# Recurrence steps with the heads in two column halves and the state used as it is; preparation products alternating between row halves

## The chip, the cores and the metric

The kernel runs on one core of a Trainium2 chip. The metric is the device time of one execution in microseconds (us). Times of engines come from one execution that the hardware profiler recorded.

## What is computed

A block of depth 2 on 512 latent and 256 context tokens (768 in all), width 1024, everything in fp32. Each layer computes a modulation from `ada_w`, a projection, then side by side an RWKV group (a recurrence in both directions over 8 heads of 64 channels, over the context and on into the latents) and a differential attention, an output projection and an MLP. The change touches the RWKV group alone:

```python
def step(state, inp):                       # one token
    r_t, w_t, k_t, v_t, kk_t, b_t = inp
    sa = jnp.einsum("bhvk,bhk->bhv", state, kk_t)
    state = (state * w_t[:, :, None, :]
             - sa[..., :, None] * b_t[:, :, None, :]
             + v_t[..., :, None] * k_t[:, :, None, :])
    y = jnp.einsum("bhvk,bhk->bhv", state, r_t)
    return state, y
...
for d, reverse in enumerate((False, True)):
    dec_c, km_c, b_c = direction_terms(kc, kkc, xwc, xac, w0[d], w_b[d], a0[d], a_b[d], k_a)
    state_c, yc = wkv_scan(state0, rc, dec_c, km_c, vc, kkc, b_c, reverse)
    _, yl = wkv_scan(state_c, r, dec, km, v, kk, bb, reverse)
```

## The kernel before

The tokens of a direction are cut in chunks of 64. A tile `n` (0 to 5) is 128 tokens of each direction `d`; a **step** `(n, j)` takes one chunk of both directions, so a layer has 12 steps and 24 calls (step and direction). Within a chunk the recurrence is a triangular system, and so it is solved by an inverse per chunk and head.

`prep_a` and `prep_b` are the **preparation** of one unit: tile `n`, direction `d`, four of the eight heads (`pp`). A unit projects the low-rank inputs (L977, out `pb`, with the zero-padded input `ltz`), makes decays by a sigmoid on GpSimd (`sg`), scans (`cs`) and exponentials, forms `BK` and `KR`, multiplies them to `G` (L1046: two PSUM banks one after the other, each the product over one half of the rows, four heads; each is evacuated by VectorE at L1048), and transposes `BK` into `BN` (L1053). `KR`, `BN` and `G` lie in one buffer `S` per tile and direction, of which there are six, so the buffer of tile n is used again by tile n+3. `relay` (L1086) sends the diagonal 32x32 blocks of `G` to DRAM (`da`).

`inv(n)` loads them as `N` and `W` (L1115, L1116), inverts all blocks of a tile at once by **elimination** (30 rounds of a product at L1100 and a sum at L1102, on GpSimd for n below 2 and on VectorE for the rest), sends the result out (`dn` L1123, `dt` L1127) and back (`TT` L1132, `Gs` L1137), and `merge(n)` fills the off-diagonal blocks of the inverse in `G`: 32 small products at L1152 and L1154, a copy `Z`, 32 products at L1160 and L1162, a copy on VectorE (L1164) and one on ScalarE (L1165).

A call of `step` on TensorE: `X` of 64 rows by 512 columns, the eight heads side by side, from `G` and the values `uv` (L1186, rows 64 to 127 of the array as contraction), plus the state's part by four products with a block-diagonal copy `sbd` of the state (L1189). ScalarE negates `X` into `xs` (L1192). The inverse in `G` times `xs` gives `us` (L1198), copied into `uv` (L1201). `BN` times `uv` gives the state's increment (L1210), VectorE adds and scales it (`st` L1213, `sc` L1215), and ScalarE copies it twice, by halves, into `sbd` (L1218). The output is summed up in rows 64 to 127 of `X`'s bank (L1226) and evacuated into `Y` (L1236, L1239). `finish` normalizes a token tile and transposes it (L1288).

Layer 0's preparation of tiles 0 and 1 and their inverses run beside the attention, the rest in `rest`: per n the inverse of n+1, the steps of n, the preparation of n+2, with TensorE matmuls of the modulation (`adar`, weights `in_ada_w` by DMA) and finished tiles' work between. This is only the order in which the code emits; a tile scheduler orders the instructions on each engine when the kernel is built, and each engine then runs its queue in that order. An fp32 matmul shows in the trace as two MATMUL records, a transpose as one.

Of the kernel before, what the change touches and what calls it, by code (L numbers as in the profile page):

```python
# [10 lines left out]
F32 = mybir.dt.float32  # L11
# [153 lines left out]
class K:  # L165
# [760 lines left out]
    def recurrence(self, l, last, es, side):  # L926
# [18 lines left out]
        ltz = [tp.tile([128, 2, 128], F32, name=self.n("ltz")) for _ in range(2)]  # L945

        for z in ltz:
            nc.gpsimd.memset(z, 0.0)
# [3 lines left out]
        sbd = one.tile([128, 2, 4, 128], F32, name=self.n("sbd"))  # L952
        nc.gpsimd.memset(sbd, 0.0)
        sc = [one.tile([128, 4, 64], F32, name=self.n("sc")) for _ in range(2)]
# [7 lines left out]
        def prep_a(n, d, pp):  # L962
# [3 lines left out]
            lt = ltz[d]  # L966
            if pp == 0:
                for a in range(2):
                    ps = slice(64 * a, 64 * a + 64)
                    nc.sync.dma_start(lt[ps, a, :], self.zd[16, ps, tok])  # L970
# [3 lines left out]
            pw = bank([128, 2, 2, 128])  # L974
# [6 lines left out]
            for p in range(2):  # L981
                nc.scalar.activation(th[:, p, :], pw[:, p, 0, :], AF.Tanh, scale=0.5,
                                     bias=self.Q(l, "w0h")[:, q + p:q + p + 1])
            for p in range(2):
                nc.scalar.activation(ta[:, p, :], pw[:, p, 1, :], AF.Tanh, scale=0.5,
                                     bias=self.Q(l, "a0h")[:, q + p:q + p + 1])
            return ld, th, ta

        def prep_b(n, d, pp, ld, th, ta):
# [51 lines left out]

            for hf in range(2):
                hs = slice(hf * 64, hf * 64 + 64)
                pgt = bank([128, 4, 128])
                for u in range(4):
                    nc.tensor.matmul(pgt[:, u, 0:nn], BK[hs, u, :], KR[hs, 2 * pp + u, 0:nn],  # L1046
                                     start=True, stop=True, skip_group_check=True)
                nc.vector.tensor_tensor(G[:, us, hf, 0:nn], pgt[:, :, 0:nn],  # L1048
# [118 lines left out]
        def step(n, j):  # L1167
            need_y = not (last and n < 2)
            final = n == 5 and j == 1
            mw = 128 if need_y else 64  # L1170
            S = []
            for d in range(2):
# [4 lines left out]
                self.gate = ld  # L1177
                KR, BN, G, dcv = sets[(n, d)]
                S.append(dict(q=q, t0=t0, uv=uv, KR=KR, BN=BN, G=G, dc=dcv))
            for d in range(2):  # L1180
                s = S[d]
                q = s["q"]
                X = s["X"] = px[d].tile([128, 512], F32, name=self.n("X"), tag=f"X{d}")
                for h in range(8):
                    w = mw if h == 0 else 64
                    nc.tensor.matmul(X[0:w, h * 64:h * 64 + 64], s["G"][64:128, h - h % 2 + q, h % 2, 0:w],  # L1186
                                     s["uv"][64:128, h, :], start=(h == 0), stop=False, skip_group_check=True)
# [4 lines left out]
                nc.scalar.mul(xs[0:64], X[0:64, :], -1.0)  # L1192
                yield
            for d in range(2):
                s = S[d]
                up = us[:, d]
                for h in range(8):
                    nc.tensor.matmul(up[(h % 2) * 64:(h % 2) * 64 + 64, h // 2, :], s["G"][:, h - h % 2 + s["q"], h % 2, 0:64],  # L1198
                                     s["xs"][:, h * 64:h * 64 + 64], start=True, stop=True, skip_group_check=True)
# [3 lines left out]
            if not final:  # L1203
                for d in range(2):
                    s = S[d]
                    q = s["q"]
                    sp = us[:, d]
                    for h in range(8):
                        hs = slice((h % 2) * 64, (h % 2) * 64 + 64)
                        nc.tensor.matmul(sp[hs, h // 2, :], s["BN"][:, h - h % 2 + q, hs], s["uv"][:, h, :],  # L1210
                                         start=True, stop=True, skip_group_check=True)
                    tt = uvp.tile([128, 4, 64], F32, name=self.n("st"), tag="st")
                    nc.vector.tensor_tensor(tt, sp, sc[d], ALU.add)  # L1213
                    dcv = s["dc"][:, q:8:2].unsqueeze(2).to_broadcast([128, 4, 64])
                    nc.vector.tensor_tensor(sc[d], tt, dcv, ALU.mult)  # L1215
                    for hf in range(2):
                        hs = slice(hf * 64, hf * 64 + 64)
                        nc.scalar.copy(sbd[hs, d, :, hs], sc[d][hs])  # L1218
                    yield
            if need_y:  # L1220
                for d in range(2):
                    s = S[d]
                    X = s["X"]
                    for h in range(8):
                        ks = slice(0, 64 if h == 0 else 128)
                        nc.tensor.matmul(X[64:128, h * 64:h * 64 + 64],  # L1226
                                         s["G"][ks, h - h % 2 + s["q"], h % 2, 64:128],
                                         s["uv"][ks, h, :], start=False, stop=(h == 7), skip_group_check=True)
# [4 lines left out]
                    yo = Yt[hp * 64:hp * 64 + 64, :]  # L1233
                    if hp not in seen:
                        seen[hp] = 1
                        nc.scalar.copy(yo, X[64:128, :])  # L1236
                    else:
                        seen[hp] = 2
                        nc.vector.tensor_tensor(yo, X[64:128, :], yo, ALU.add)  # L1239
# [4 lines left out]
        def finish(ti):  # L1244
# [40 lines left out]
            yield  # L1285
            pt = bank([128, 4, 128])
# [450 lines left out]
```

## Time and profile before

| what | value |
|---|---|
| three runs, median (lowest to highest) | 2450.8 us (2442.71 to 2458.3) |
| profiled execution: time; span; mean granted clock | 2465.64 us; 2463.9 us; 0.933 |
| busy over the span: PE, DVE, ACT, POOL | 92%, 62%, 48%, 33% |
| recurrence of layer 0, 494 to 763 us | 269 us, granted clock 0.90 |
| recurrence of layer 1, 1758 to 2062 us | 304 us, granted clock 0.77 |

The recurrence stretches reach from the end of the attention beside which the first tiles are prepared to the last products of the output projection that stand between steps. PE is TensorE's matmuls, DVE is VectorE, ACT ScalarE, POOL GpSimd, SP the queue that issues most DMAs.

### The profile page before, as it was taken

Reading aid. Unit: us, or ns where it says so; the run is one execution under the profiler, and the core shown is the slowest. Engines: PE = TensorE matmul, PEld = TensorE weight load, DVE = VectorE, ACT = ScalarE, POOL = GpSimd, SP = SyncE. Lnnn points to the kernel's source line nnn. Section 1 sums busy time; section 2 is a strip of 40 time slices with the busy share of each in tenths; the row PEclk is TensorE's granted clock in tenths of the full one; section 3 lists DMA queues with packets and bytes.
Section 4 is the critical chain, followed back from the end, with each engine's and each line's share of the span. In section 5 each row is a group of like instructions: output and inputs, shape, how many; then the busy total and the mean of one; then the engine's idle time right before and its main releaser. Section 6 shows DMA issues by size and latency. Waiting matters only on the chain.

```text
span 2463.9 us, 43744 instructions
## 1 busy us (share of the span) xinstructions
PE 2273.2 (92%) x17150; PEld 1919.2 (78%) x17150; DVE 1516.6 (62%) x2629; ACT 1173.8 (48%) x2393; POOL 806.8 (33%) x1048
## 2 busy tenths in 40 slices
PE   6999998799989999999999989999989978999997
PEld 5887887677768988888888877788767758888886
DVE  5456458558654665555555646657556564778784
ACT  4345547554534543344343535547444444555452
POOL 1212324832111333333330422423641131553530
PEclk8999998798899999999999999999678879999998
DMA  7543535386687422221112354434566663423230
GB/s 270 154 129 94 133 110 140 74 228 172 148 208 236 152 77 69 69 69 61 60 61 85 124 164 122 122 108 115 148 158 158 166 161 137 161 91 117 87 119 35
DMA packets 291630, 313.67 MB, mean 127 GB/s; under 512 B 139680, under 2 KB 220896, under 8 KB 291424
## 3 DMA queue, kind: packets, MB, share of 16 engines
q1 hardware_dynamic: 280320, 284.66, 38.6%
q0 software_dynamic: 10240, 23.08, 5.0%
q8 instruction: 135, 2.21, 0.4%
q10 hardware_dynamic: 864, 3.15, 0.3%
q14 instruction: 71, 0.58, 0.1%
HBM read 257.04 MB, written 53.77 MB: 126 GB/s over the span
## 4 chain that ended last, share of the span: by engine, by line
PE 68%; DMA 10%; DVE 9%; ACT 4%; issue 3%; SPq 2%; POOL 2%; POOLq 0%; DVEq 0%; ACTq 0%
PE pf L351 31%; PE pu L351 15%; PE po L351 4%; DMA raw<-in_ada_w 2%; PE pb L1046 2%; PE po L832 2%; DMA TT<-dt 2%; PE X L1186 1%; PE pb L977 1%; PE adar L265 1%; PE sc L795 1%; DVE wl L1497 1%; PE X L1226 1%; DVE nm L797 1%; PE X L1189 1%
## 5 line engine op out<-in xcount | busy, mean ns | idle before, releaser
L1497 DVE TENSOR_TENSOR wl<-raw,wh 128x1024 fp32r<-128x1024 f32 x170 | 255.8, 1507 | 125.6 <-ACT wh L1496 124.8
L351 PE MATMUL pf<-hl,wh 128*128 128x512 f32 (+1 forms) x832 | 282.1, 342 | 0.0
L351 PE MATMUL pf<-hh,wh 128*128 128x512 f32 (+1 forms) x832 | 280.5, 342 | 0.5 <-ACT hh L397 0.5
L351 PE MATMUL pf<-hh,wl 128*128 128x512 f32 (+1 forms) x832 | 275.7, 342 | 0.0
L1496 ACT ACTIVATE wh<-raw 128x1024 fp32r<-128x1024 f32 x170 | 179.2, 1058 | 162.0 <-PE pf L351 143.9
L351 PE MATMUL pf<-wh,fah 128*128 128x512 f32 x570 | 225.3, 398 | 11.5 <-DVE fu L1630 7.2
L351 PE MATMUL pu<-hh,wh 128*128 128x512 f32 (+1 forms) x632 | 223.5, 354 | 4.8 <-DVE t L557 1.7
L351 PE MATMUL pf<-wl,fah 128*128 128x512 f32 x570 | 225.0, 396 | 0.7 <-DVE wl L1497 0.7
L351 PE MATMUL pf<-wh,fal 128*128 128x512 f32 x570 | 222.8, 397 | 1.8 <-DVE fal L1597 1.8
L351 PE MATMUL pu<-hh,wl 128*128 128x512 f32 (+1 forms) x632 | 218.1, 346 | 4.4 <-DVE wl L340 4.4
L351 PE MATMUL pu<-hl,wh 128*128 128x512 f32 (+1 forms) x632 | 217.8, 345 | 0.0
L797 DVE TENSOR_REDUCE nm<-sc 128x1 f32<-128x768 f32 (+1 forms) x160 | 132.6, 842 | 79.2 <-PE sc L795 78.5
L351 PEld LDWEIGHTS pf<-hl,wh 128*128 128x128 f32 x832 | 156.6, 188 | 20.0 <-DVE hl L399 0.2
L351 PEld LDWEIGHTS pf<-hh,wl 128*128 128x128 f32 x832 | 156.0, 188 | 20.0
L351 PEld LDWEIGHTS pf<-hh,wh 128*128 128x128 f32 x832 | 155.3, 188 | 20.4 <-ACT hh L397 0.8
L799 ACT ACTIVATE e<-sc,nm 128x768 f32<-128x768 f32 (+1 forms) x160 | 130.7, 821 | 53.7 <-DVE nm L797 44.3
L321 POOL TENSOR_TENSOR rs<-ms,pw 128x1 f32<-128x1 f32 (+2 forms) x60 | 56.8, 948 | 286.3 <-DVE ms L319 284.5
L351 PEld LDWEIGHTS pu<-hh,wh 128*128 128x128 f32 x632 | 121.0, 191 | 23.8 <-DVE t L557 2.3
L351 PEld LDWEIGHTS pf<-wh,fah 128*128 128x128 f32 x570 | 107.7, 189 | 38.9 <-ACT fah L1596 13.7
L1630 DVE TENSOR_TENSOR acc<-pf,acc 128x512 f32<-128x512 f32 x155 | 104.2, 682 | 53.9 <-PE pf L351 53.3
L351 PEld LDWEIGHTS pu<-hh,wl 128*128 128x128 f32 x632 | 120.7, 191 | 19.5 <-DVE wl L340 5.3
L351 PEld LDWEIGHTS pu<-hl,wh 128*128 128x128 f32 x632 | 120.8, 191 | 14.2 <-issue 1.7
(262 smaller groups left out, 5644.1 us busy)
## 6 DMA issues: line engine op xcount, KB each, us to landing
raw<-in_w_ff SPq DMA_DIRECT2D x128, 512.0 KB, 3.7
raw<-in_ada_w SPq DMA_DIRECT2D x96, 512.0 KB, 5.8
raw<-in_w_in SPq DMA_DIRECT2D x52, 512.0 KB, 4.6
ld<-zd SPq DMA_DIRECT2D x40, 384.0 KB, 3.9
ks<-qd POOLq DMA_DIRECT2D x64, 192.0 KB, 5.8
zd<-zr SPq DMA_DIRECT2D x22, 384.0 KB
raw<-in_w_out SPq DMA_DIRECT2D x16, 512.0 KB, 5.9
qs<-qd POOLq DMA_DIRECT2D x32, 192.0 KB, 6.0
```

What stands on the lines that cost most here:

```text
L265: nc.tensor.matmul(acc[32 * g:32 * g + 32, :], self.sc[:, 2 * kp + k, :], raw[:, k, g * 128:g * 128 + 128], start=(kp + k == 0), stop=(kp ...
L321: nc.gpsimd.tensor_tensor(r, m, self.pw1.to_broadcast([128, cols]), ALU.pow)
L351: nc.tensor.matmul(out, a, b, start=(start and i == 0 and j == 0), stop=(i == n - 1 and j == 2), skip_group_check=not start)
L795: nc.tensor.matmul(sc[:, k0:k1], qs[:, br, tk], ks[:, br, k0:k1], start=True, stop=True)
L797: nc.vector.tensor_reduce(nm, sc, AX.X, ALU.max, negate=True)
L799: nc.scalar.activation(ee, sc, AF.Exp, bias=nm, accum_out=ls[:, br:br + 1])
L832: nc.tensor.matmul(po, pT[:, k * 128:k * 128 + 128], vn[:, k, h * 64:h * 64 + 64], start=(k == 0), stop=(k == nk - 1))
L977: nc.tensor.matmul(pw[:, p, :, :], wab[:, d, cs], lt, start=True, stop=True, skip_group_check=True)
L1046: nc.tensor.matmul(pgt[:, u, 0:nn], BK[hs, u, :], KR[hs, 2 * pp + u, 0:nn], start=True, stop=True, skip_group_check=True)
L1496: nc.scalar.activation(hi, src, AF.Copy)
L1497: nc.vector.tensor_tensor(lo, src, hi.bitcast(F32), sub)
L1630: nc.vector.tensor_tensor(d, p, d, add)
```

## The change

`lt` replaces the padded `ltz`: one DMA instead of two, no zeros, and four products with a contraction of 64 rows into two banks instead of two products of 128 rows and 256 columns into one. The `G` products run over the heads outside and the two row halves inside, so that both banks are held at once. `sbd` and its copies are gone: `from_state` multiplies the state `sc` as it is, head by head, in 64x64 products that alternate between the quadrants of the array, once for `X` and once more for the output. `X` is 128 rows by 4 heads, even heads in the upper column half, odd in the lower; its `G` product contracts all 128 rows, with `uv[0:64]` zeroed by a new memset on GpSimd, so it reads the rows of `G` that hold the inverse too. `xs` is two muls of 64x256. `us` and the state's increment lie in `X`'s bank, the output in a bank of its own (`Yb`). `finish` transposes by sixteen 64x64 products.

```diff
-        ltz = [tp.tile([128, 2, 128], F32, name=self.n("ltz")) for _ in range(2)]
+        lts = [tp.tile([128, 128], F32, name=self.n("lt")) for _ in range(2)]
...
+            pw = [bank([128, 2, 128]) for _ in range(2)]
             for p in range(2):
                 cs = slice((pp + p) * 128, (pp + p) * 128 + 128)
-                nc.tensor.matmul(pw[:, p, :, :], wab[:, d, cs], lt, start=True, stop=True, skip_group_check=True)
+                for a in range(2):
+                    ps = slice(64 * a, 64 * a + 64)
+                    nc.tensor.matmul(pw[a][:, p, :], wab[ps, d, cs], lt[ps, :], start=True, stop=True,
+                                     skip_group_check=True)
...
+            pgs = [bank([128, 4, 128]) for _ in range(2)]
+            for u in range(4):
+                for hf in range(2):
+                    hs = slice(hf * 64, hf * 64 + 64)
+                    nc.tensor.matmul(pgs[hf][:, u, 0:nn], BK[hs, u, :], KR[hs, 2 * pp + u, 0:nn],
+                                     start=True, stop=True, skip_group_check=True)
...
+                nc.gpsimd.memset(uv[0:64], 0.0)
...
+            def from_state(out, s, c0):
+                for h in range(8):
+                    hs = half(h)
+                    nc.tensor.matmul(out[hs, h // 2, :], s["KR"][hs, h - h % 2 + s["q"], c0:c0 + 64], s["old"][hs, h // 2, :],
+                                     start=False, stop=False, skip_group_check=True)
...
-                for p in range(4):
-                    nc.tensor.matmul(X[0:mw, p * 128:p * 128 + 128], s["KR"][:, 2 * p + q, 0:mw], sbd[:, d, p, :],
-                                     start=False, stop=False, skip_group_check=True)
+                    nc.tensor.matmul(X[half(h), 0, h // 2, :], s["G"][:, h - h % 2 + s["q"], h % 2, 0:64],
+                                     s["uv"][:, h, :], start=(h < 2), stop=False, skip_group_check=True)
+                from_state(X[:, 0], s, 0)
...
-                    for hf in range(2):
-                        hs = slice(hf * 64, hf * 64 + 64)
-                        nc.scalar.copy(sbd[hs, d, :, hs], sc[d][hs])
...
+                        nc.tensor.matmul(Y[half(h), h // 2, :], s["G"][:, h - h % 2 + s["q"], h % 2, 64:128],
+                                         s["uv"][:, h, :], start=(h < 2), stop=False, skip_group_check=True)
+                    from_state(Y, s, 64)
```

The order on the engines changes far beyond these lines. TensorE before, layer 0, at the merge of tile 2 (it writes `S_5374` and `S_5501`, the two directions of tile 2; X_6648 and X_6771 are this same tile's):

```order
L1189 MATMUL X_6648<-sbd_3609,S_5374 128x128 x4
L265 MATMUL adar_6685<-raw_6716,sc 32x128 x3
L1186 MATMUL X_6771<-uv_6646,S_5501 64x64 x3
L1046 MATMUL pb_6851<-S_4135,BK_6823 128x128 x4
L1046 MATMUL pb_6857<-S_4135,BK_6823 128x128 x4
L1189 MATMUL X_6771<-sbd_3609,S_5501 128x128 x4
L287 MATMUL adat_7084<-cst,row_6726 128x128
L977 MATMUL pb_6874<-ltz_3603,wab_3600 128x256 x2
L1152 MATMUL pg_5905<-TT_5898,S_5374 32x32
```

TensorE with the change, at the merge of the same tile (it writes `S_5401` and `S_5538`; `S_4146` and `S_4387` are tile 1, and X_6064 and X_6174 are tile 1's):

```order
L1186 MATMUL Yb_5857<-sc_5663,S_3920 64x64 x8
L1186 MATMUL X_6064<-sc_5825,S_4146 64x64
L265 MATMUL adar_6085<-raw_6096,sc 32x128 x7
L265 MATMUL adar_6085<-raw_6106,sc 32x128 x8
L265 MATMUL adar_6085<-raw_6116,sc 32x128 x8
L975 MATMUL pb_6130<-lt_3602,wab_3600 128x128
L975 MATMUL pb_6131<-lt_3602,wab_3600 128x128
L1045 MATMUL pb_6162<-S_3659,BK_6156 128x128 x4
L1193 MATMUL X_6174<-uv_6061,S_4387 64x64 x2
L1152 MATMUL pg_5988<-TT_5981,S_5401 32x32
```

The merge of tile n stood at the X products of tile n's first step, and now stands at those of tile n-1's first step, one tile earlier; all merges from tile 2 on stand so in layer 0, and nearly so in layer 1.

VectorE before, layer 0, about the merge copy of tile 2 (`W_6462` is the elimination of tile 3, BK and cs belong to the preparation of later tiles):

```order
L1100 TENSOR_TENSOR pr_6494<-W_6462,N_6461 128x105
L1102 TENSOR_TENSOR W_6462<-W_6462,pr_6494 128x5x21
L1100 TENSOR_TENSOR pr_6497<-W_6462,N_6461 128x120
L1102 TENSOR_TENSOR W_6462<-W_6462,pr_6497 128x6x20
L1100 TENSOR_TENSOR pr_6500<-W_6462,N_6461 128x114
L1102 TENSOR_TENSOR W_6462<-W_6462,pr_6500 128x6x19
L1294 TENSOR_TENSOR ysq_6664<-ysq_6664,frk_6662 128x512
L1100 TENSOR_TENSOR pr_6503<-W_6462,N_6461 128x126
L1164 COPY S_5374<-pg_5940 32x16x32
L1018 SCALAR_TENSOR_TENSOR cs_7462<-scm_3606,sg_7459 128x260
L1034 TENSOR_TENSOR BK_6995<-ta_6878,xi_6989 128x4x2x32
L1035 TENSOR_TENSOR BK_6995<-th_6877,xi_6989 128x4x64
```

VectorE with the change, the end of the elimination of tile 2 (`W_5876`) and the merge copy behind it:

```order
L1102 TENSOR_TENSOR W_5876<-W_5876,pr_5965 128x15x2
L1100 TENSOR_TENSOR pr_5968<-W_5876,N_5875 128x15
L1102 TENSOR_TENSOR W_5876<-W_5876,pr_5968 128x15
L1017 SCALAR_TENSOR_TENSOR cs_6217<-scm_3604,sg_6214 128x260
L1030 TENSOR_TENSOR th_6136<-th_6136,ld_6128 128x256
L1048 TENSOR_TENSOR S_3659<-pb_6162,cst 128x4x128
L1031 SCALAR_TENSOR_TENSOR ta_6137<-ta_6137,ld_6128 128x256
L1034 TENSOR_TENSOR BK_6227<-th_6136,xi_6221 128x4x64
L1033 TENSOR_TENSOR BK_6227<-ta_6137,xi_6221 128x4x64
L1048 TENSOR_TENSOR S_3659<-pb_6163,cst 128x4x128
L1164 COPY S_5401<-pg_6023 32x16x32
```

and further on the end of the preparation of tile 3 (`S_3920`) and the start of tile 3's elimination (`W_6611`):

```order
L1017 SCALAR_TENSOR_TENSOR cs_6902<-scm_3604,sg_6899 128x260
L1048 TENSOR_TENSOR S_3920<-pb_6372,cst 128x4x128
L1030 TENSOR_TENSOR th_6335<-th_6335,ld_6327 128x256
L1031 SCALAR_TENSOR_TENSOR ta_6336<-ta_6336,ld_6327 128x256
L1034 TENSOR_TENSOR BK_6912<-th_6335,xi_6906 128x4x64
L1033 TENSOR_TENSOR BK_6912<-ta_6336,xi_6906 128x4x64
L1048 TENSOR_TENSOR S_3920<-pb_6373,cst 128x4x128
L1241 TENSOR_TENSOR Y_5701<-Yb_6404,Y_5701 128x256
L1100 TENSOR_TENSOR pr_6616<-W_6611,N_6610 128x30
```

The elimination of tile n+1 was interleaved with the merge of tile n and with the preparation of tile n+2; now it stands behind that merge and behind its own tile's last three units of preparation (two of them between rows not shown here), nearly undivided.

TensorE with the change, `G` products of another unit (`pb_6243` and `pb_6244` are the two banks of one unit):

```order
L1204 MATMUL X_6064<-xs_5148,S_4146 64x64 x8
L1204 MATMUL X_6174<-xs_5149,S_4387 64x64 x2
L1045 MATMUL pb_6243<-S_3659,BK_6227 128x128 x4
L1045 MATMUL pb_6244<-S_3659,BK_6227 128x128 x4
L1053 MATMUL pb_6255<-cst,BK_6227 128x128 x4
L1204 MATMUL X_6174<-xs_5149,S_4387 64x64 x6
L1215 MATMUL X_6064<-uv_6058,S_4146 64x64 x2
```

The code emits the products of the two banks in turn; here the built order has all four of one and then all four of the other, as before at `pb_6851` and `pb_6857`.

## Rows read from the trace of the kernel before

**Rows 1.** Windows: busy us (instructions) per engine, granted clock, DMA share.

```profile
494.00:763.00 269.00, 240.41 (x3478) 192.92 (x3477) 169.22 (x461) 128.52 (x304) 66.12 (x113) 0.90 0.77 198
...
1758.00:2062.00 304.00, 260.51 (x3339) 215.35 (x3337) 167.99 (x453) 129.14 (x301) 88.18 (x178) 0.77 0.57 147
```

**Rows 2.** Chain of waits by line, the two recurrence stretches.

```profile
by line: DMA raw<-in_ada_w 10.1%; DMA TT<-dt 7.3%; PE pb L1046 6.5%; PE X L1226 6.1%; PE adar L265 5.8%; PE X L1186 4.1%; DMA raw<-in_w_out 3.5%; DMA S<-gd 3.3%; PE pb L977 3.2%; DMA da<-S 3.1%; PE X L1189 3.0%; issue 3.0%; PE us L1198 3.0%
...
by line: PE X L1186 8.5%; PE pb L1046 6.0%; PE adar L265 5.7%; PE X L1189 5.4%; PE po L351 5.3%; issue 4.8%; PE pb L977 4.7%; DMA TT<-dt 4.7%; DMA raw<-in_ada_w 4.3%; PE X L1226 4.1%; DMA S<-zd 3.9%; PE us L1198 3.5%; PE us L1210 2.8%; DVE 
```

**Rows 3.** Chain in order of time: start us, us, what (TensorE calls).

```profile
495.39 1.09 PE X L1189 x8
...
497.34 1.32 PE X L1186 x16
...
504.66 0.61 PE us L1198 x16
...
506.96 0.61 PE X L1226 x8
...
1760.33 1.89 PE X L1186 x16
```

**Rows 4.** Groups by line, whole program: busy us, mean ns.

```profile
L1102 DVE TENSOR_TENSOR W<-W,pr 128x30 f32<-128x30 f32 (+7 forms) x240 | 66.0, 275 | 5.5
L1100 DVE TENSOR_TENSOR pr<-W,N 128x30 f32<-128x30 f32 (+7 forms) x240 | 65.7, 274 | 15.5 <-DMA N<-da 10.3
```

**Rows 5.** Chain in order of time, from a relay to a merge.

```profile
566.46 5.18 DMA da<-S
...
574.71 6.68 DMA N<-da
...
637.57 3.99 DMA dn<-W
...
642.03 3.27 DMA TT<-dt
...
645.35 0.24 PE pg L1152 x2
```

**Rows 6.** Timeline of ScalarE, last copy of merges: start us, us.

```profile
530.70 0.58 ACT L1165 COPY S<-pg 32x512 f32<-32x512 f32 x1 [5.54 <-DVE S L1164]
...
733.74 0.58 ACT L1165 COPY S<-pg 32x512 f32<-32x512 f32 x1
...
1861.26 0.58 ACT L1165 COPY S<-pg 32x512 f32<-32x512 f32 x1 [4.27 <-DVE S L1164]
...
2024.90 0.58 ACT L1165 COPY S<-pg 32x512 f32<-32x512 f32 x1
```

**Rows 7.** Timeline of TensorE at a merge.

```profile
646.53 0.26 PE L1154 MATMUL pg<-TT,S 32*32 32x32 f32 x1
646.54 0.26 PE L1152 MATMUL pg<-TT,S 32*32 32x32 f32 x1
646.60 0.24 PE L1154 MATMUL pg<-TT,S 32*32 32x32 f32 x1
```

**Rows 8.** Timeline of TensorE, start of preparation units in layer 1.

```profile
1708.88 1.02 PE L977 MATMUL pb<-ltz,wab 128*128 128x256 f32 x4
...
1714.47 1.03 PE L977 MATMUL pb<-ltz,wab 128*128 128x256 f32 x4
...
1744.45 1.88 PE L977 MATMUL pb<-ltz,wab 128*128 128x256 f32 x4 [1.53 <-DVE S L1048]
...
1751.54 2.02 PE L977 MATMUL pb<-ltz,wab 128*128 128x256 f32 x4
```

**Rows 9.** Waits of TensorE: us in total, times, longest (stretches 494:770, 1760:2055).

```profile
PE adar L265 <- DMA raw<-in_ada_w: 15.0, 11, 2.6
PE X L1189 <- ACT sbd L1218: 3.1, 2, 2.2
...
PE pg L1152 <- DMA TT<-dt: 10.4, 5, 5.4
```

More of the change, by code (lines that the diff above doesn't have):

```diff
@@ L951, in recurrence @@
         nc.gpsimd.memset(scm[:, 0:260:65], 0.0)
-        sbd = one.tile([128, 2, 4, 128], F32, name=self.n("sbd"))
-        nc.gpsimd.memset(sbd, 0.0)
-        sc = [one.tile([128, 4, 64], F32, name=self.n("sc")) for _ in range(2)]
+        state = lambda d: one.tile([128, 4, 64], F32, name=self.n("sc"), tag=f"sc{d}", bufs=2)
+        sc = [state(d) for d in range(2)]
         for s in sc:
@@ L1040, in prep_b @@
             yield
-            for hf in range(2):
-                hs = slice(hf * 64, hf * 64 + 64)
[L1044 to L1048, printed above, removed]
+            pgs = [bank([128, 4, 128]) for _ in range(2)]
[4 more added lines that the diff above has]
+                                     start=True, stop=True, skip_group_check=True)
+            for hf in range(2):
+                nc.vector.tensor_tensor(G[:, us, hf, 0:nn], pgs[hf][:, :, 0:nn],
                                         msk[:, 0:nn].unsqueeze(1).to_broadcast([128, 4, nn]), ALU.mult)
@@ L1222, in step @@
                     s = S[d]
-                    X = s["X"]
+                    Y = yp.tile([128, 4, 64], F32, name=self.n("Yb"), tag="Yb")
                     for h in range(8):
[L1225 to L1228, printed above, removed]
+                        nc.tensor.matmul(Y[half(h), h // 2, :], s["G"][:, h - h % 2 + s["q"], h % 2, 64:128],
+                                         s["uv"][:, h, :], start=(h < 2), stop=False, skip_group_check=True)
+                    from_state(Y, s, 64)
                     ti, hp = s["t0"] // 128, (s["t0"] // 64) % 2
@@ L1287, in finish @@
             for p in range(4):
-                nc.tensor.transpose(pt[:, p, :], Yt[:, p * 128:p * 128 + 128], self.ident)
+                for hp in range(2):
+                    for hf in range(2):
+                        hs = slice(hf * 64, hf * 64 + 64)
+                        c0 = hp * 256 + p * 64
+                        nc.tensor.matmul(pt[hs, p, hp * 64:hp * 64 + 64], Yt[hs, c0:c0 + 64], self.ident[hs, hs],
+                                         start=True, stop=True, skip_group_check=True)
             o1 = sq.rearrange("p (j t) -> p j t", j=4)
@@ L1308, in rest @@
             uvp = self.pool(es, "uvp", 2)
-            xsd = [uvp.tile([128, 512], F32, name=self.n("xs"), bufs=1) for _ in range(2)]
+            xsd = [uvp.tile([128, 2, 4, 64], F32, name=self.n("xs"), bufs=1) for _ in range(2)]
             for x in xsd:
@@ L1314, in rest @@
             late["pg"] = lambda shape: pg.tile(shape, F32, name=self.n("pg"), tag="g")
-            us = self.pool(es, "pus", 1, PSUM).tile([128, 2, 4, 64], F32, name=self.n("us"))
+            yp = self.pool(es, "pyb", 1, PSUM)
             pms.append(self.pool(es, "pmr", 1, PSUM))
```

51 lines of the change are left out of this document (21 added, 30 removed).

## The prediction

> **What bounds the kernel now.** I read the busy times of the two recurrence stretches first [rows 1]. TensorE is busy 240 of 269 us in layer 0 and 261 of 304 us in layer 1, at granted clocks of 0.90 and 0.77; VectorE is busy 169 and 168 us, ScalarE some 129, GpSimd under 90. So TensorE looks like the bound. The chain of waits says less [rows 2]: no TensorE line has more than 8.5% of a stretch, and in layer 0 the first two entries are DMAs, one of them (TT<-dt) the last transfer of an inverse. The waits of TensorE name the same two sources, a modulation weight (15.0 us) and TT (10.4 us in layer 1) [rows 9]. Third, the last copies of the merges [rows 6]: from tile 1 to tile 5 they take 530.7 to 733.7 in layer 0, and from tile 2 to tile 5 1861.3 to 2024.9 in layer 1, which is most of each stretch. Steps can't run ahead of these. So there are two clocks in the stage, TensorE's work and the loop of preparation, relay, elimination and merge, and the question is which of them the new order leaves in charge.
>
> **What the change takes off TensorE.** A call's X was 1.32 us (products from one row half into one column half) and 1.09 us (block-diagonal state) [rows 3]. The new G product has the shape of the us product, alternating column halves over 128 rows: 0.61 us [rows 3]. The state's product, 64x64 in alternating quadrants, has no row. Its bounds are 0.3 us (half of 0.61, if the two row halves run beside each other) and 1.32 us (nothing beside anything, as in the old X); I take 0.61, since alternating column halves at least is the same. X falls from 2.41 to 1.22 us. The output falls from twice 0.61 [rows 3] to 0.61 for G, and rises by the second state product, another 0.61: no change. The relief is 1.19 us a call, 24 calls a layer: 29 us in layer 0 and, at a granted clock of 0.77, 37 us in layer 1, 66 together (27 to 83 by the two bounds). At half clock the old X piece was 1.89 us [rows 3], so the relief grows there too.
>
> The preparation should gain by products that alternate row halves, but the built order undoes most of it: where one G product follows another, it changes the bank in 88 of 305 places (39 of 313 before), and the low-rank products change in 48 places of 118. I give it 0 to -5 us. The dropped sbd copies free ScalarE of two copies a call; TensorE waited for them 3.1 us in layer 0 [rows 9], so that is all they are worth. The added memset of uv on GpSimd costs nothing while GpSimd is three quarters idle in layer 0 and 70% idle in layer 1 [rows 1]; without that cover, what stands behind it on the queue is the sigmoid and KR of a later unit. It must wait for a free uv buffer, as the uv load on SP does. From a gain of nothing to a loss of 1 us in each of 24 steps is the bound; I take 0. The finish's sixteen small transposes against four change under 1 us a tile.
>
> One thing in the order speaks against the alternation in the array. At a merge, a product at L1154 and one at L1152 start 0.01 us apart, from different row groups of 32 and into the same bank, and the next pair follows 0.06 us later, though one record takes 0.24 us [rows 7]. So here row groups run beside each other in one bank. The Trainium skill, TensorEngine Tiling (Array Packing), Restrictions and Gotchas, says that different row tiles can't access the same PSUM bank at the same time; from_state does precisely that, and by this rule its products would run one after the other. What that would give is the third rival.
>
> **What the change puts on the path.** In the built order the merge of tile n stood beside the X of tile n, which did not read the inverse; the new X contracts all 128 rows, reads what the merge writes, and the merge stands one tile earlier on TensorE. On VectorE the elimination of tile n+1 no longer overlaps the merge of tile n: behind the merge copy come the evacuations of three units' G (in layer 0; 2.5, 1.5 and 3 units in layer 1), and only then the 60 operations of the elimination, nearly undivided. A queue runs in order, so merge, units, relay, elimination and merge follow one another. One turn of this loop:
> - three units. Units began 5.6 us apart in the prologue of layer 1 at full clock [rows 8]. The first one's head stands ahead of the merge copy, so three take between two pitches, 11.2, and three, 16.8: 14.
> - relay. da 5.18 and N 6.68 make 11.9, and from the start of the one to the landing of the other it was 14.9 [rows 5]: 13.
> - elimination: (66.0 + 65.7) / 8 tiles = 16.5 [rows 4], if nothing interrupts it.
> - from dn's start to the first merge product, 637.57 to 645.35: 7.8 [rows 5].
> - merge: two rounds of 32 pairs at some 0.055 us [rows 7], 3.6, and two copies of 0.58 [rows 6]: 4.8.
>
> That is 56 us (50 to 64 with the ends). Layer 0: merge 1 stays at 530; to merge 2 it takes elimination, transfers and merge, 29 us, and up to 13 for the relay, so 36; three turns are 168. Merge 5 comes at 734 instead of 733.7. Layer 1: three times 42 for the turn without units and 7 units at 4.7 are 159 between merges 2 and 5, where it was 163.6: -4. During these turns TensorE has room: a tile's two steps need 4 calls of 3.7 us (X 1.22, us 0.61, increment 0.6, output 1.22) and four units. So the relief falls where TensorE then waits.
>
> Behind the last merge stands now one tile's two steps more: 4 calls at 3.7 us, 15 us of TensorE, less what overlapped the old tail, 733.7 to 763. The bounds are 1 (it fills waits for modulation weights, 15.0 us in all) and 15; I take 8 in each layer.
>
> **Sum.** Layer 0 0 + 8, layer 1 -4 + 8, sbd and preparation -0 to -5 with the one tail that they touch, which I set against the longer wait of X behind its merge: +12 to +13 us. On the profiled execution 2465.6 + 13 = 2478.6; the median of the runs shown is 2450.8 / 2465.64 = 0.994 of that, so 2464 us: half a per cent slower, within the 1% (24.5 us) that a measurement of this kernel can tell from no change. This case is **no change**, chance 0.41.
>
> **Rivals.**
> *TensorE stays in charge, and the relief passes to the end.* For it: 89% and 86% busy, and X's two lines with 7.1% and 13.9% of the chains [rows 2]: 19 + 42 = 61 us, of which 1.19/2.41 goes, 30, and 3 for the sbd waits. 2432.6 x 0.994 = 2418. If all 66 pass, 2385. Against it: the loop above doesn't contain these lines, and its turn must come to 50 us or less. Chance 0.25.
>
> *The units between merge and elimination are slow.* A unit now holds two banks at once for the low-rank products and two for G, out of three in the stage and two in the prologue, so the next unit can't start before both are evacuated, and VectorE's evacuations stand behind the merge copy. Units at half clock began 7.1 us apart [rows 8]. At that pitch each of 16 units costs 2.4 us more, 39 us: (2478.6 + 39) x 0.994 = 2502. It is slower by over 1% from some 0.8 us more a unit on, a pitch of 5.5. Against it: that pitch was at half clock, and 5.6 at full clock lies about at the point where it decides. Chance 0.30.
>
> *Products from two row halves into one bank don't overlap.* The state's product then costs 1.32 instead of 0.61, 88 times 0.71, 62 us: the relief is gone. Since the loop is in charge, only the calls behind the last merge and the first X of each of ten tiles pay: 8 calls x 1.4 and 10 x 1.4 at both products, 25 us: 2489. The merge's rows speak against it [rows 7]: chance 0.04.
>
> **How the numbers follow.** The likeliest is 2464. The range leaves out the full relief and the slow units' worst: 2405 to 2510. Its low end lies between the chain's gain and the full relief, its high end above units at 7.1 us. Faster by over 1% (under 2426) is most of the first rival and the fast end of the loop, 0.26; slower by over 1% (over 2475) most of the other two and the slow end of the loop, 0.35; between them 0.39.
>
> **What would show it.** Right: X as two pieces of some 0.6 us each; TensorE's busy time in the stretches down by some 30 and 37 us, and its idle time up by about as much; the elimination in 17 us without other work between; merges of layer 0 56 us apart, of which 14 are units; two tiles' steps behind the last merge; TensorE's wait for TT or VectorE's wait for the merge larger. Wrong: merges 37 to 45 us apart and stretches shorter by 15 us or more, which would mean that the units run ahead of the merge copy after all. If from_state's 16 records take over 1 us, the bank rule holds. If the granted clock of layer 1's stretch falls below 0.77, a longer time there says nothing on the loop.

## The result, and the profile after

The changed kernel takes 2625.4 us (median of four runs, 2620.9 to 2632.3), before 2449.1 (2442.7 to 2458.3): the ratio is 1.073, with an interval of 1.069 to 1.076. The profiled execution is 2632.3 us with a span of 2630.5, 166.6 longer than before, at a mean granted clock of 0.872 instead of 0.933.

The page of the changed kernel, its busy times and the granted clock in 40 slices:

```profile
PE 2353.8 (89%) x18646; PEld 1992.7 (76%) x18646; DVE 1521.6 (58%) x2629; ACT 1145.7 (44%) x2353; POOL 817.0 (31%) x1090
...
PEclk8999997576657999999999999998565668999999
```

TensorE is busy longer, not shorter (2273.2 us before), and the clock falls in slices 7 to 13 and 28 to 34, which hold the two recurrences with the preparation ahead of them. The same views as [rows 1] for the recurrences, from the first X to the last output (365 us against 269 in layer 0, 282 against 287 in layer 1, where the first X now waits for a merge):

```profile
510.00:875.00 365.00, 274.58 (x4060) 225.13 (x4060) 168.25 (x459) 110.11 (x279) 76.26 (x143) 0.67 0.49 128
1924.00:2206.00 282.00, 216.09 (x3452) 182.13 (x3448) 145.68 (x402) 92.96 (x232) 55.82 (x116) 0.68 0.49 123
```

The clock is 0.67 and 0.68, near the lower level of TensorE's two (0.5 of full speed, 1.2 GHz). VectorE is busy in layer 0 for as long as before (168 us) and ScalarE for less, in 96 us more. The chain of waits of layer 0, answering [rows 2]:

```profile
by line: PE pb L1045 9.7%; DMA raw<-in_ada_w 8.2%; DVE pr L1100 6.2%; DVE W L1102 6.2%; PE pb L975 4.6%; issue 4.4%; DMA N<-da 4.1%; PE X L1215 3.5%; DMA dt<-R 2.9%; PE adar L265 2.9%; PE X L1204 2.8%; PE pb L1053 2.5%; PE pb L1283 2.5%; DM
```

The two products of X (L1193, L1186) are no longer among the first lines; what is called X there is the state's increment (L1215) and `us` (L1204), which lie in X's bank now. In their place stand the G products and the low-rank products of the preparation (L1045, L975), and the elimination (L1100, L1102) with N<-da: the loop. TensorE's calls, answering [rows 3] (chain in order of time; start us, us, what):

```profile
537.72 2.06 PE pb L1045 x16
...
829.00 0.62 PE X L1193 x16
829.62 0.61 PE X L1186 x16
```

At full clock the new X is 0.62 (G) and 0.61 us (state), as forecast. The G products of a unit take 2.06 us where the built order alternates the row halves (all 16 records), and twice 2.00 where it does not (597.04 and 599.66 in the turn shown below), both at half clock. So alternating does halve them, where it takes place. The last copies of merges, answering [rows 6] (tiles 2 to 5 of layer 0, tiles 2 and 5 of layer 1):

```profile
586.17 0.58 ACT L1165 COPY S<-pg 32x512 f32<-32x512 f32 x1
...
664.76 0.58 ACT L1165 COPY S<-pg 32x512 f32<-32x512 f32 x1
...
743.84 0.58 ACT L1165 COPY S<-pg 32x512 f32<-32x512 f32 x1
...
810.41 0.58 ACT L1165 COPY S<-pg 32x512 f32<-32x512 f32 x1 [2.40 <-DVE S L1164]
...
1974.32 0.58 ACT L1165 COPY S<-pg 32x512 f32<-32x512 f32 x1 [2.51 <-DVE S L1164]
...
2170.12 0.58 ACT L1165 COPY S<-pg 32x512 f32<-32x512 f32 x1 [3.04 <-DVE S L1164]
```

In layer 0 the turns from merge 2 on are 79, 79 and 67 us; in layer 1 the three from tile 2 to 5 come to 196 us, where it was 164. One turn, from the merge of tile 2 to the first products of the merge of tile 3, in the chain (the longest pieces; answers [rows 5]), and the first and the last operation of its elimination:

```profile
585.34 1.04 PE pb L1053 x4
...
597.04 2.00 PE pb L1045 x8
...
599.66 2.00 PE pb L1045 x8
...
608.57 2.01 PE pb L1045 x8
...
611.70 1.95 DMA da<-S
...
615.65 5.52 DMA N<-da
...
645.65 2.13 DMA dt<-R
...
650.61 5.08 DMA raw<-in_ada_w
...
655.74 1.08 PE adar L265 x16
```

```profile
621.29 0.19 DVE L1100 TENSOR_TENSOR pr<-W,N 128x30 f32<-128x30 f32 x1 [7.98 <-DMA N<-da]
...
643.39 0.17 DVE L1102 TENSOR_TENSOR W<-W,pr 128x15 f32<-128x15 f32 x1
```

The units take 585.3 to 611.3, 26 us, and the chain there is TensorE almost throughout, at half clock. Relay and loads take 10 us, the elimination 22.3 (the state's additions, the output's evacuations and a finish stand between its operations). From its end to the merge copy at 664.8 it is 21 us: the transfers, and then the two rounds of the merge's products, which stand 8 us apart, since adar products that wait for a modulation weight and products of a step, a finish and a unit are queued between them:

```profile
650.58 0.31 PE L1152 MATMUL pg<-TT,S 32*32 32x32 f32 x2 [3.84 <-DMA TT<-dt]
...
655.74 1.08 PE L265 MATMUL adar<-raw,sc 128*32 128x128 f32 x16 [2.60 <-DMA raw<-in_ada_w]
...
661.16 0.26 PE L1160 MATMUL pg<-S,Z 32*32 32x32 f32 x1
```

VectorE's waits in layer 0 name the loop directly (us in total, times, longest):

```profile
DVE S L1164 <- PE pg L1162: 36.1, 5, 15.7
DVE pr L1100 <- DMA N<-da: 33.9, 4, 9.9
```

Before, over 494 to 763 us, they were

```profile
DVE S L1164 <- PE pg L1162: 10.6, 3, 9.1
...
DVE pr L1100 <- DMA N<-da: 3.0, 2, 2.1
```

Now they are 70 us of layer 0 in which VectorE, with its evacuations and scans behind it, stands still. In layer 1 only the wait for the relay grew, from 7.3 to 33.3 us; the one for the merge did not (29.3 before, 25.3 now).

### The profile page after: what moved, and what is told of

It is laid out like the page before. It is cut to its first block, busy times and chain, and to the rows that moved or that the text cites. A ratio compares the mean times of both kernels' runs of the same rounds, so it can differ in the third digit from the quotient of the medians.

```text
span 2630.5 us, 46692 instructions
## 1 busy us (share of the span) xinstructions
PE 2353.8 (89%) x18646; PEld 1992.7 (76%) x18646; DVE 1521.6 (58%) x2629; ACT 1145.7 (44%) x2353; POOL 817.0 (31%) x1090
## 4 chain that ended last, share of the span: by engine, by line
PE 69%; DVE 11%; DMA 8%; ACT 3%; issue 3%; POOL 3%; SPq 2%; ACTq 0%; DVEq 0%; POOLq 0%
PE pf L351 29%; PE pu L351 15%; PE po L351 4%; PE pb L1045 4%; PE po L832 3%; DMA raw<-in_ada_w 2%; DVE pr L1100 2%; DVE W L1102 2%; PE pb L975 2%; PE sc L795 2%; DMA N<-da 2%; PE adar L265 1%; PE ptr L815 1%; DVE wl L1505 1%; PE pb L1053 1%
## 5 line engine op out<-in xcount | busy, mean ns | idle before, releaser
L265 PE MATMUL adar<-raw,sc 128*32 128x128 f32 x1536 | 89.2, 375 | 77.4 <-DMA raw<-in_ada_w 40.1
L1045 PE MATMUL pb<-S,BK 64*128 64x128 f32 (+1 forms) x768 | 143.3, 391 | 8.3 <-DVE BK L1033 2.8
L1045 PEld LDWEIGHTS pb<-S,BK 64*128 64x128 f32 x768 | 124.5, 284 | 20.6 <-issue 9.0
```

Of the source, the lines that this page charges most:

```text
L265: nc.tensor.matmul(acc[32 * g:32 * g + 32, :], self.sc[:, 2 * kp + k, :], raw[:, k, g * 128:g * 128 + 128], start=(kp + k == 0), stop=(kp ...
L1045: nc.tensor.matmul(pgs[hf][:, u, 0:nn], BK[hs, u, :], KR[hs, 2 * pp + u, 0:nn], start=True, stop=True, skip_group_check=True)
```

## Experiments

Fourteen kernels ran; each ratio is against runs of the kernel before on the same chip.

**Parts of the change.** Four kernels leave out parts. `step_only` has the low-rank products and the G products of before, `no_lowrank` only the low-rank products of before, `no_g` only the G products of before:

```diff
-            pw = [bank([128, 2, 128]) for _ in range(2)]
+            pw = bank([128, 2, 2, 128])
...
-                    nc.tensor.matmul(pw[a][:, p, :], wab[ps, d, cs], lt[ps, :], start=True, stop=True,
...
+                nc.tensor.matmul(pw[:, p, :, :], wab[:, d, cs], lt, start=True, stop=True, skip_group_check=True)
...
-            pgs = [bank([128, 4, 128]) for _ in range(2)]
-            for u in range(4):
-                for hf in range(2):
...
+            for hf in range(2):
...
+                pgt = bank([128, 4, 128])
+                for u in range(4):
```

`prep_only` has both new pieces of preparation in the kernel before.

> The new steps and the new finish, with the preparation as it was before (padded low-rank input, G products one bank after the other). In the built order the eliminations on VectorE are again interleaved with the preparation, though X still reads what the merge writes. Theory A (the loss is the serial loop of merge, units, relay and elimination in the built order, which needs the new low-rank products and the new steps together): 2420 to 2480 us. Theory B (X behind the merge costs the time): 2580 us or more. Theory C (the half-row products of the preparation lower the granted clock and lose the time by themselves): 2440 to 2460.

Measured: 2487.6 us, ratio 1.018 (1.013 to 1.023).

> The new preparation (low-rank products into two banks, G products over two banks at once) with the steps and the finish as before. In the built order the eliminations are interleaved with the preparation. Theory A: 2440 to 2500 us, with units in the prologues a little further apart. Theory B: 2440 to 2460. Theory C: 2580 us or more, with a granted clock of 0.6 to 0.7 in the recurrence of layer 0.

Measured: 2470.6 us, 1.012 (1.006 to 1.019).

> The change without its low-rank part: padded input and one bank again; G products alternate, steps and finish are new. In the built order eliminations and preparation are interleaved. Theory A: 2430 to 2490 us, merges of layer 0 some 40 to 55 us apart. Theory B: 2600 or more. Theory C: about half of the loss, 2530.

Measured: 2491.4 us, 1.018 (1.013 to 1.023).

> The change without its alternating G products: one bank after the other again; the low-rank products go to two banks, steps and finish are new. In the built order the eliminations stand undivided behind the units, as with the whole change. Theory A: 2600 to 2640 us, the whole loss. Theory B: 2600 or more too. Theory C: about half of the loss, 2530.

Measured: 2618.3 us, 1.071 (1.065 to 1.076).

The whole loss is there when the low-rank products and the new steps are both there, and only then. It goes exactly with the built order: of these four only `no_g` has the undivided eliminations. Theory A's ranges hold `prep_only` and `no_g`; `step_only` and `no_lowrank` lie 8 and 1 us above theirs, and the merges of `no_lowrank` in layer 0 are 85, 33, 50 and 40 us apart instead of 40 to 55. Theory C is out (the new preparation alone costs 1.2%). Theory B, X behind the merge, is left with at most 1.8%.

**Is the rest X behind the merge?** `behind_merge` adds to the kernel before only that X reads the inverse's rows:

```diff
+                nc.gpsimd.memset(uv[0:64], 0.0)
...
-                    nc.tensor.matmul(X[0:w, h * 64:h * 64 + 64], s["G"][64:128, h - h % 2 + q, h % 2, 0:w],
-                                     s["uv"][64:128, h, :], start=(h == 0), stop=False, skip_group_check=True)
+                    nc.tensor.matmul(X[0:w, h * 64:h * 64 + 64], s["G"][:, h - h % 2 + q, h % 2, 0:w],
+                                     s["uv"][:, h, :], start=(h == 0), stop=False, skip_group_check=True)
```

> The kernel before with one thing added: the G product of X contracts all 128 rows, with the lower half of uv zeroed on GpSimd, so that X reads what the merge writes; its result is the same. Nothing else of the change is in it. Theory E (X behind the merge is what makes the new steps alone 1.8% slower): 2470 to 2500 us, with a longer tail behind the last merge. Rival F (something else in the new steps does, the second state product, the two muls or the transposes): 2445 to 2460.

Measured: 2447.4 us, 1.000 (0.998 to 1.002). Theory E falls for the program as a whole: with the dependence and the memset it takes no longer. What E expected of the tail is there, though. The built order is another one here too, the last merges come 24 and 35 us sooner than before, and from the last merge to the end of the last output's evacuation it is 40 us in layer 0 and 37 in layer 1, against 30 and 23 before. Layer 0's last merge and last evacuation:

```profile
709.28 0.58 ACT L1165 COPY S<-pg 32x512 f32<-32x512 f32 x1
...
748.55 0.69 DVE L1240 TENSOR_TENSOR Y<-X,Y 64x512 f32<-64x512 f32 x1
```

**Other orders of the same instructions.** `late_inv` and `late_merge` emit the inverse or the merge later, and change nothing else:

```diff
-                elif n < 5:
-                    self.now(inv(n + 1))
                 for j in range(2):
+                    if j == 1 and 0 < n < 5:
+                        self.now(inv(n + 1))
```

```diff
-            if n > 1:
-                merge(n)
-                yield
...
+                if 0 < n < 5:
+                    merge(n + 1)
                 if n < 4:
                     prep_until(n + 2)
```

> The whole change, instruction for instruction, but the inverse of tile n+1 is emitted after the first step of tile n instead of ahead of it, which gives another built order: in most turns the first part of the elimination of tile n+1 stands ahead of the merge of tile n, and the preparation runs a tile further ahead. Theory A (the serial loop in the order is the cause): turns of 45 to 60 us instead of 67 to 79, 2470 to 2540 us. Rival D (the products themselves, their half-row tiles or their two banks, are the cause whatever the order): 2600 or more.

Measured: 2558.6 us, 1.045 (1.041 to 1.050).

> The whole change, but the merge of tile n+1 alone is emitted after both steps of tile n. In the built order the merges stand two steps later on TensorE, and some eliminations are still undivided between units and merge, others not. Theory A: between the two, 2500 to 2580 us, with the undivided turns as long as in the whole change and the others shorter. Rival D: 2600 or more.

Measured: 2558.0 us, 1.045 (1.040 to 1.050). Both give back some 67 us with no instruction changed, so the order matters by itself. `late_merge` lies in A's range, `late_inv` 19 us above it: its turns from merge 1 on are 74, 62, 70 and 40 us in layer 0 (42, 79, 79 and 67 with the whole change), and its eliminations are still nearly undivided (19 to 22 us each). So the order costs, but which part of it, the undivided elimination, the early merge or the units between them, is not told apart.

**Order against product, two by two.** `two_banks_full` is the change with low-rank products of 128 rows again, but in two banks:

```diff
-                    nc.tensor.matmul(pw[a][:, p, :], wab[ps, d, cs], lt[ps, :], start=True, stop=True,
+                    nc.tensor.matmul(pw[a][:, p, :], wab[:, d, cs], lt[:, a, :], start=True, stop=True,
                                      skip_group_check=True)
```

> The whole change, but the low-rank products contract 128 rows again, with the zero-padded input, and still go to two banks. In the built order eliminations and preparation are interleaved. Theory A: 2470 to 2510 us, as without the low-rank part. Rival D, if holding two banks for them is what costs: 2580 or more; if the half-row tiles are: 2490 too, so this run speaks on the banks alone.

Measured: 2458.1 us, 1.005 (1.003 to 1.008). Two banks are not what costs. It is faster than A expected, and it has the new steps and the new finish, so the 1.8% of `step_only` are not a price of these as such; what they come from was not followed further. But here the order changed with the products. `narrowed` takes this order and then makes each product half a row high in its place, after the order is fixed; `half_padded` has the half-row products of the padded input and its own order, and `widened` that order with full rows:

```diff
                     nc.tensor.matmul(pw[a][:, p, :], wab[:, d, cs], lt[:, a, :], start=True, stop=True,
...
+                    b.instructions[k] = replace(i, ins=[rows(lt, 64 * a, 64), rows(w, 64 * a, 64)], tile_size=(64, 128),
+                                                tile_position=(64 * a, 0))
```

> Instruction for instruction the order of two_banks_full on every engine (eliminations interleaved with the preparation), but each of the 192 low-rank products then contracts the 64 rows that are not zero, as in the change: other than the padded input, these are the instructions of the change. Theory A (the order alone costs the time): 2450 to 2480 us. Theory D2 (the half-row low-rank products cost it, by the array or by the granted clock that they leave behind): 2560 to 2640. Theory G (both, half each): 2500 to 2540.

Measured: 2472.8 us, 1.009 (1.005 to 1.012).

> The change with the padded input, low-rank products of 64 rows into two banks: the same instructions as narrowed, in the order that they give by themselves (from tile 3 on the eliminations undivided behind the units). Theory A: 2590 to 2640 us. Theory D2: 2560 to 2640 too. Theory G: 2590 to 2640.

Measured: 2590.2 us, 1.057 (1.053 to 1.061).

> Instruction for instruction the order of half_padded on every engine (eliminations undivided behind the units), but each low-rank product then contracts all 128 rows of the padded input, as in two_banks_full. Theory A: as half_padded within 1%, 2580 to 2640 us. Theory D2: 2455 to 2500. Theory G: 2530 to 2580.

Measured: 2580.7 us, 1.053 (1.048 to 1.057).

| order | full rows | half rows |
|---|---|---|
| eliminations interleaved | 2458 | 2473 |
| eliminations undivided from tile 3 on | 2581 | 2590 |

Down a column only the order differs, along a row only the product. By the ratios, the order is worth 4.8% in both columns, some 117 us, and half rows 0.3 to 0.4%, 8 to 10 us, with intervals that overlap. (The medians of the table give 123 for the order in the left column, but 2458 comes from another chip, on which the kernel before was 6 us faster.) Theory A holds, D2 and G fall. The whole change, 2625, lies another 35 us above `half_padded`; it has the unpadded input and an order that is undivided from tile 2 on, and the share of each is not shown. The merges of the two kernels with the same instructions, tiles 3, 4 and 5 of layer 0, first `narrowed`:

```profile
641.48 0.58 ACT L1168 COPY S<-pg 32x512 f32<-32x512 f32 x1 [2.17 <-DVE S L1167]
...
667.75 0.58 ACT L1168 COPY S<-pg 32x512 f32<-32x512 f32 x1 [2.96 <-DVE S L1167]
...
735.21 0.58 ACT L1168 COPY S<-pg 32x512 f32<-32x512 f32 x1 [8.14 <-DVE S L1167]
```

then `half_padded`:

```profile
622.38 0.58 ACT L1169 COPY S<-pg 32x512 f32<-32x512 f32 x1 [3.58 <-DVE S L1168]
...
713.95 0.58 ACT L1169 COPY S<-pg 32x512 f32<-32x512 f32 x1 [2.51 <-DVE S L1168]
...
777.04 0.58 ACT L1169 COPY S<-pg 32x512 f32<-32x512 f32 x1 [2.66 <-DVE S L1168]
```

From tile 3 on, where its order is serial, `half_padded` takes 155 us for two turns, against 94. (From merge 1 to merge 5 it is 236 against 192, since the first turns of `narrowed` are longer.) VectorE's waits over their recurrences of layer 0, first `narrowed`, then `half_padded`:

```profile
DVE pr L1103 <- DMA N<-da: 4.7, 2, 3.8
...
DVE S L1167 <- PE pg L1165: 2.5, 2, 2.2
```

```profile
DVE S L1168 <- PE pg L1166: 34.4, 3, 15.8
DVE pr L1104 <- DMA N<-da: 29.8, 4, 11.3
```

7 us against 64. The 57 us between are about as much as the two recurrences differ by (280 and 343 us from the first us product to the last output).

**Why a turn is so long, and where TensorE's relief goes.** Three kernels queue each G product of a unit behind the one ahead of it, so that the built order keeps the alternation: `after_chain` in the changed kernel, `g_chain` in the kernel before, `g_chain_step` in `two_banks_full`.

```diff
+            prev = None
             for u in range(4):
                 for hf in range(2):
                     hs = slice(hf * 64, hf * 64 + 64)
-                    nc.tensor.matmul(pgs[hf][:, u, 0:nn], BK[hs, u, :], KR[hs, 2 * pp + u, 0:nn],
-                                     start=True, stop=True, skip_group_check=True)
+                    with tc.issue_after(prev.ins) if prev else ExitStack():
+                        prev = nc.tensor.matmul(pgs[hf][:, u, 0:nn], BK[hs, u, :], KR[hs, 2 * pp + u, 0:nn],
+                                                start=True, stop=True, skip_group_check=True)
```

> The whole change, with each G product of a unit queued behind the one ahead of it, so that on TensorE the row halves alternate in every unit, as the code says and the built order did not. The eliminations stand undivided behind the units as in the whole change, so the loop is the same, but a unit's G products take about half of their TensorE time (2.06 us where they alternated, 4.0 where they did not, both at half clock). Theory H (the turn is longer than forecast since TensorE does the units between merge and elimination one after the other at half clock): turns of 55 to 68 us instead of 67 to 79, 2530 to 2590 us. Rival I (the turn is made of waits of queues and DMAs, TensorE's share is small): 2605 or more.

Measured: 2581.8 us, 1.055 (1.050 to 1.061).

> The kernel before with one thing alone: the G products of a unit alternate between the row halves, two banks at once, and each is queued behind the one ahead of it, so that the built order keeps the alternation. Eliminations and preparation stay interleaved. If the alternation halves the products' TensorE time (48 units by about 1.1 us at full clock) and half of that passes to the end: 2410 to 2430 us; if holding two banks takes it back or TensorE is not what bounds: 2440 to 2460.

Measured: 2453.9 us, 1.003 (1.000 to 1.005).

> The new steps and finish, the low-rank products of 128 rows in two banks, and the G products alternating in the built order too. Eliminations and preparation are interleaved. If the relief of the steps and of the units passes to the end once the loop is not in its way: 2390 to 2430 us, the fastest of all. If the loop of inverses bounds even when interleaved: 2440 to 2470, no better than two_banks_full.

Measured: 2502.1 us, 1.021 (1.018 to 1.025).

The groups of G products, of `after_chain`, of `g_chain` and of the changed kernel (busy us, mean ns):

```profile
L1047 PE MATMUL pb<-S,BK 64*128 64x128 f32 (+1 forms) x768 | 100.7, 373 | 13.1 <-DVE S L1050 3.7 <-POOL S L1037 2.9 <-ACT th L981 2.2
```

```profile
L1048 PE MATMUL pb<-S,BK 64*128 64x128 f32 (+1 forms) x768 | 73.6, 315 | 6.8 <-ACT ta L985 2.9 <-DVE BK L1034 1.8 <-DVE ri L806 0.8
```

```profile
L1045 PE MATMUL pb<-S,BK 64*128 64x128 f32 (+1 forms) x768 | 143.3, 391 | 8.3 <-DVE BK L1033 2.8 <-POOL S L1037 2.2 <-DVE ri L806 1.6
```

The alternation takes 43 us of TensorE's busy time from the change, and the time falls by 44: theory H's range. But the turns don't all follow: in layer 0 they are 56, 72 and 64 (79, 79 and 67), in layer 1 78, 53 and 66 (75, 57 and 64), so three of six lie in H's range, and the order of the first tiles changed with it (merge 1 at 534 instead of 544). That busy time and time fall by the same amount may be chance. In the kernel before, where L1046 was busy 108.2 us, a relief of 35 us makes nothing faster. With the new steps (`g_chain_step`) the time is 2.1% above before and 1.6% above `two_banks_full`, in yet another order; both of its forecasts fail, and why is not shown. So TensorE's time in the units is hidden in the interleaved order of before; that it counts in the serial loop fits `after_chain` and is not shown.

## Why the prediction was wrong

It forecast 2464 us, no change, with 0.35 for slower and 2510 as the upper end; it is 2625. The step that failed is the sum of one turn of the loop (56 us, measured 79), above all its term for three units (14 us, measured 26). The sum foresaw some 12 us on the profiled execution, and the span grew by 167. Of the 155 between, the turns have 99 (63 in layer 0, 37 in layer 1), the tails 42 and the start 13.

**Right: the mechanism.** The part "what the change puts on the path" named it: the merge one tile earlier, the elimination undivided behind three units, a loop in which nothing overlaps. The two by two runs show for nearly the same kernel that the order, and not the arithmetic, takes the time. Also right: X falls to 1.23 us a call at full clock, with the state's product at 0.61 (a choice between 0.3 and 1.32), and products from two row halves into one bank do not run one after the other: from_state's neighbours differ in row half and write other partitions of one bank, and its 16 records take 0.61 us at full clock, under the 1 us that was set and under the 1.32 of the old X. The Trainium skill, TensorEngine Tiling (Array Packing), Restrictions and Gotchas, says that different row tiles can't access one bank at the same time; for products into different partitions this trace doesn't bear it out, and the measurement decides. The relief of TensorE does not pass to the end: `g_chain` shows that for the units, and `two_banks_full` for the steps, where TensorE is busy 152 us with X and the output instead of 197 in an interleaved order, and the time is 0.5% longer. The first rival (faster, 0.25) falls with it.

**Wrong: the sum of a turn.** Its terms were taken from rows in which that step ran alone or at full clock, and in the loop the price of all but the relay was higher. One turn of layer 0, forecast and measured (merge 2 to merge 3):

| term | forecast | measured |
|---|---|---|
| three units | 14 | 26 |
| relay and loads | 13 | 10 |
| elimination | 16.5 | 22.3 |
| transfers, merge | 12.6 | 21 |
| turn | 56 (50 to 64) | 79 |

The units went wrong by most: TensorE did them back to back at half clock. In the chain of these 26 us are 9.9 us of G products (three times 2.06 would be 6.2 with full alternation), 5.7 of low-rank products, 3.1 of transposes and 6.5 of the steps' own products, for which the prediction had said that TensorE has room. An estimate from the clock alone: at full clock 26 us of such work would be 13, so the clock is about the whole miss of this term. The slow-units rival had this (a pitch of 7.1 us at half clock) and priced it at 7 us a turn; it was 12. That rival, 2502, was the nearest. What half clock costs on the whole can't be told apart from the order here: no run has the serial order at full clock. The rows on it: in the changed kernel's layer 0 the clock goes from 0.83 over 0.59 to 0.50 while TensorE's busy time goes from 12.5 and 13.6 of 20 us (the longest wait there, 6.0 us, is for TT, the inverse's last transfer) to 20.0 of 20 in the units:

```profile
550.00:570.00 20.00, 12.50 (x236) 10.60 (x236) 16.66 (x64) 2.70 (x7) 1.93 (x5) 0.83 0.41 134
570.00:590.00 20.00, 13.62 (x209) 11.78 (x209) 5.65 (x11) 9.33 (x26) 2.89 (x7) 0.59 0.61 150
590.00:610.00 20.00, 20.00 (x129) 16.83 (x129) 10.17 (x22) 8.40 (x23) 4.82 (x11) 0.50 0.22 56
```

In layer 1's stretch the clock fell to 0.68, below 0.77, and by the prediction's own sign the longer time there then says nothing on the loop.

**Wrong: the terms around the loop.** "Merge 1 stays at 530" was 544: a part for which the prediction had no term at all. It begins on GpSimd, where the elimination of tile 0 takes 53.6 us (430.6 to 484.2) instead of 38.4 (428.7 to 467.1): the operations of preparation that stand in its order there wait, most of all for ScalarE (us in total, times, longest, 430 to 485 us; no such wait before).

```profile
POOL sg L1013 <- ACT th L981: 9.1, 3, 4.9
```

So merge 0 is at 507.8 instead of 484.7, and the first X, which now stands behind it, at 510 instead of 494. The tail was given 8 us in each layer; from the last merge to the last output it is 64 us in layer 0 (29 before), and to the last transpose 54 in layer 1 (31 before), 35 and 23 more, though the pieces of the calls there take 0.6 us where the clock is full. With the turns (merge 1 to 5 of layer 0 +64, merge 2 to 5 of layer 1 +32) and the start (+13 to merge 1 of layer 0) these make 167 us, which is what the span grew by; all other stretches add up to nothing.

**Not settled: X behind the merge as a price.** The tail was argued from X's dependence on the merge. `behind_merge` has that dependence, and its program takes no longer; but its tails are 10 and 13 us longer than before, near the 8 that were given, and earlier merges make up for it. By the same measure the changed kernel has 66 and 36: layer 1's tail is as long as with the dependence alone, and what lengthens layer 0's further was not told apart.

**Not foreseen at all:** which edit makes the order. It is the half-row low-rank products that tip it, and only together with the new steps; by themselves these products cost under half a per cent. Why the scheduler answers to them so was not tried.

## What to carry to other kernels

Read the built order of a changed kernel as an edit of its own, and price it as a loop: follow one item through all queues and ask what must end before the next can start. When two versions differ in arithmetic and in order, give one the other's order before judging the arithmetic; here, of a loss of 7% a kernel with the same products but a padded input has 5.7%, and 4.8% are shown to be order alone, its effect on the granted clock included. A term of such a loop is to be priced at the clock and in the company that the loop itself will have, not from the row in which it ran best.

## What was not expected of the hardware

TensorE being less busy in a stretch did not go with a higher clock: in the serial order it is busy 259 of 343 us at 0.72 (`half_padded`, layer 0), in the interleaved one, with the same instructions, 230 of 280 us at 0.83 (`narrowed`):

```profile
494.00:837.00 343.00, 259.25 (x4103) 212.22 (x4103) 170.68 (x463) 112.60 (x286) 79.42 (x149) 0.72 0.56 144
```

```profile
498.00:778.00 280.00, 229.76 (x4129) 187.34 (x4127) 172.74 (x471) 117.16 (x292) 81.76 (x147) 0.83 0.72 188
```

And row halves were worth alternating only where products of the two follow each other in turn: 16 records of G products took 2.06 us alternating, and 8 records 2.00 us in one half, so 16 took 4.0, both at the lower clock (0.50).
